# A row-maximum kernel that skips NaNs: VectorE write-back of two quarter rows in tile 62, and a rewritten choice of the engine that writes back

## The chip, the cores and the metric

The kernel runs on one core of a Trainium2 chip. The metric is device time in microseconds; the kernel before takes 1250.19 us (median of three runs, 1250.16 to 1250.23). Engines are named as in the profile: ACT is ScalarE, POOL is GpSimd, DVE is VectorE, SP is SyncE, which issues the DMAs. TensorE has no work.

## What is computed

```python
batch, seq, dim = 32, 2048, 2048
x = np.random.randn(batch, seq, dim).astype(np.float32)
x[np.random.rand(batch, seq, dim) < 0.1] = np.nan
np.nanmax(x, axis=-1).astype(np.float32)
```

There are 65,536 rows of 2048 floats, 536.87 MB in all, and one float per row comes out. Each of the 128 partitions gets 512 whole rows.

## The kernel before

**Tiles.** A tile is up to 7 rows per partition (`WIDE`), that is 28 quarter rows of 512 elements (`Q`), 14336 floats per partition and 7168 KB over the 128 partitions. The table `TILES` lists 75 tiles. An entry has three lists of quarter rows: the loads (one DMA each), the steps and the maxima. Tile n lies in `xt0`, `xt1` or `xt2`, in turn, and the load of a tile waits for the last maximum of the tile that had the buffer before it (line 482, `free`). SP issues the loads in the order of the table (line 240).

**Steps.** A NaN must lose against every number before VectorE takes a maximum. Only the upper 16 bits of each float are touched, seen as a signed integer with a stride of two. First ACT computes a 16-bit key of every element (`act`, line 265, called on line 419): the upper half is mirrored at `TOP` = 0x7F7F with a Prelu whose steep negative branch sends a NaN so far that it comes back as minus infinity. The keys go to one of three key buffers `kt0` to `kt2` of 6144 elements (`KEYS`, `NKEYS`); a step that doesn't fit behind the earlier one takes the next key buffer, and then ACT waits until the keys in it have been written back. Then a second engine mirrors the keys again and writes them over the upper halves in `xt`: the write-back. A positive number in a step is written back by POOL (`pool`, line 275), a negative one by ACT (`release`, line 392, which issues a second ACTIVATE with the function Copy). `[9, 12, -7]` thus has three keys on ACT, two write-backs on POOL and one on ACT. A tuple puts several write-backs behind one key instruction. A float only says when ACT's write-back is issued, or, if positive, that the part joins the one before it.

The line that decides between the engines is 431, `back, wait, c = c < 0, isinstance(c, float), int(abs(c)) * Q`, and line 435, `if back:`.

**Maxima.** DVE takes the maximum of each finished row (`TENSOR_REDUCE`, lines 285 and 458) as soon as the write-backs that cover it are done. Where a maximum needs one write-back of each engine, `joints` (line 90) gives the two a semaphore of their own, so that DVE waits once.

**Order.** Every engine does its instructions in the order in which the loop over the tiles issues them; nothing is scheduled later. In the profile, an instruction's line is that of its helper: L269 is `act`, L279 is `pool`, L286 is `dve`, L245 is a load. Keys read `kt<-xt`, write-backs read `xt<-kt`. DVE's results go to `acc` for the first 60 tiles, then to `lead`. At the end DVE and POOL turn rows without any number to NaN (lines 288 and 300), and SP stores the results.

Of the 75 tiles, the first 57 are mostly `[7, 9, 12]`, with one `[9, 12, -7]` in every eight up to tile 41. Tiles 59 to 61 are `[8, 8, 8, -4]` (the last with the 4 in a tuple), tile 62 is `[7, 10, 11]`, and from tile 63 on most tiles have one or more negative numbers. The last ten are loaded in ever smaller pieces.

One name matters for the change: `tile_nanmax_kernel` begins with aliases, among them line 205, `ACT = mybir.ActivationFunctionType`.

Of the kernel before, what the change touches and what calls it, by code (L numbers as in the profile page):

```python
# [8 lines left out]
D = 2048  # L9

Q = D // 4
# [21 lines left out]
    + [([28], [7, 10, 11], [12, 16])]  # L33
    + [([28], [8, 8, 8, -4], [8, 8, 8, 4])] * 2
# [25 lines left out]

ALONE = (65,)

KEYS = 3 * D
NKEYS = 3

# [6 lines left out]
TOP = 0x7F7F  # L72
NAN = 0x7FC0
LOW = -128

EDGE = TOP + 0.25
# [2 lines left out]


def total(pieces):
    return sum(sum(map(abs, p)) if isinstance(p, tuple) else abs(p) for p in pieces)


def with_last(c):

    return isinstance(c, float) and c > 0


def joints(pieces, reds):  # L90

    flat = []
    at = 0
    for step, parts in enumerate(pieces):
        for c in parts if isinstance(parts, tuple) else (parts,):  # L100

            if with_last(c):
                flat[-1] = (flat[-1][0], at + abs(c), False, step)
            else:
                flat.append((at, at + abs(c), c < 0, step + isinstance(c, float)))
            at += abs(c)
    needs = []
    done = 0
    for n in reds:
        over = [i for i, (a, b, _, _) in enumerate(flat) if a < done + n and b > done]  # L110
        done += n
        pools = [i for i in over if not flat[i][2]]
        backs = [i for i in over if flat[i][2]]
        if pools and backs and flat[pools[-1]][3] > flat[backs[-1]][3]:
            backs = []
        needs.append(pools[-1:] + backs[-1:])
    pairs = {}
    for need in needs:
        if len(need) == 2 and all(sum(i in n for n in needs) == 1 for i in need):
            for i in need:  # L120
                pairs[i] = tuple(need)
    return pairs
# [61 lines left out]
def kernel(  # L184
# [15 lines left out]
    nc = tc.nc  # L200
    P = nc.NUM_PARTITIONS
    f32, i32 = mybir.dt.float32, mybir.dt.int32
    i16, u16 = mybir.dt.int16, mybir.dt.uint16
    ALU = mybir.AluOpType
    ACT = mybir.ActivationFunctionType
# [12 lines left out]
    def sbuf(name, width, dtype):  # L218
        return nc.alloc_sbuf_tensor(name, [P, width], dtype).ap()
# [5 lines left out]
    xts = [sbuf(f"xt{i}", WIDE * D, i32) for i in range(BUFS)]  # L225
    kts = [sbuf(f"kt{i}", KEYS, u16) for i in range(NKEYS)]
    acc0 = sbuf("acc", early, f32)

    def maxima(lo, hi):

# [23 lines left out]
    with tc.tile_critical():  # L254
        xg = xr[P * rows[-1] : P * (rows[-1] + rows[0])].rearrange("(p s) d -> p (s d)", p=P)
        ahead = []
        base = 0
# [7 lines left out]
    def act(deps, pair=None, **kw):  # L265
        return order.add(
            "act",
            nc.scalar,
            lambda: nc.scalar.activation(**kw),  # L269
            deps,  # L270
            lane=pair,
            joint=pair is not None,
        )
# [11 lines left out]
    def dve(deps, do, **kw):  # L285
        return order.add("dve", nc.vector, lambda: do(**kw), deps)  # L286
# [36 lines left out]
    clock = 0  # L323
# [3 lines left out]
        return list({back: e for back, _, e in sorted(uses, key=lambda u: u[1])}.values())  # L327

    key = 0
    used = KEYS  # L330
    number = 0
    stores = []
# [3 lines left out]
    for gi, (s, g) in enumerate(zip(rows, GROUPS)):  # L336
# [6 lines left out]
        acc = maxima(first, first + s)  # L343
        base = 0
        for loads, pieces, reds in g:
            assert sum(loads) == total(pieces) == sum(reds)
            xt, before = xts[number % BUFS], free[number % BUFS]
            number += 1
            landed = []
            at = 0  # L350
            for c in loads:
                c *= Q
                if ahead:
                    e = ahead.pop(0)
# [4 lines left out]
            clean = []  # L359
# [15 lines left out]
            def cleaned(a, b, k, i, e):  # L375

                nonlocal clock
                clock += 1
                both = [(a, b, k, flat[i] < 0, clock)]
                if i in pairs:  # L380
                    if pairs[i] not in half:
                        half[pairs[i]] = both
                        return
                    both += half.pop(pairs[i])
                for a, b, k, back, when in both:
                    kfree[k].append((back, when, e))
                    clean.append((a, b, e))
# [4 lines left out]
            def release():  # L392
                for a, b, k, kp, e, i in held:
                    e = act(
                        [e],
                        name(i),
                        out=xt[:, a:b].bitcast(i16)[:, 1::2],
                        in_=kp,
                        func=ACT.Copy,
                        bias=float(TOP),  # L400
                        scale=-1.0,
                    )
                    cleaned(a, b, k, i, e)
                held.clear()

            for parts in pieces:
                parts = parts if isinstance(parts, tuple) else (parts,)
                c = int(sum(map(abs, parts))) * Q
                here = [l for a, b, l in landed if a < at + c and b > at]
                kold = []  # L410
                if used + c > KEYS:
                    key = (key + 1) % NKEYS
                    used = 0
                    kold, kfree[key] = last(kfree[key]), []
                    assert all(k != key for q in half.values() for _, _, k, _, _ in q)
                    if at + c == sum(loads) * Q and number not in ALONE:

                        kold = kold + last(kfree[(key + 1) % NKEYS])
                e_key = act(
                    here + kold,  # L420
                    out=kts[key][:, used : used + c],
                    in_=xt[:, at : at + c].bitcast(i16)[:, 1::2],
                    func=ACT.Prelu,
                    bias=EDGE,
                    scale=-1.0,
                    alpha=float(TOP - LOW) / (EDGE - NAN),
                )
                release()
                for c in parts:
                    on = more.pop(0)  # L430
                    back, wait, c = c < 0, isinstance(c, float), int(abs(c)) * Q
                    kp = kts[key][:, used : used + c]
                    used += c
                    at += c
                    if back:
                        held.append((at - c, at, key, kp, e_key, piece))
                        if not wait or at == sum(loads) * Q:
                            release()
                    else:
                        group.append((at - c, used - c, key))  # L440
                        if not on:
                            assert all(k == key for _, _, k in group)
                            lo, klo, _ = group[0]
                            e = pool(
                                [e_key],
                                name(piece),
                                out=xt[:, lo:at].bitcast(i16)[:, 1::2],
                                in0=kts[key][:, klo:used],
                                scalar1=-1.0,
                                scalar2=float(TOP),  # L450
                                op0=ALU.mult,
                                op1=ALU.add,
                            )
                            group = []
                            cleaned(lo, at, key, piece, e)
                    piece += not on
                    open_ = [h[0] for h in held + group] + [p[0] for q in half.values() for p in q]
                    while reds and done + reds[0] <= min([at] + open_):
                        n = reds.pop(0)


                        lo = done - 1 if done % D else done
                        done += n
                        row = (base + lo) // D
                        if done % D:
                            m, to = 1, xt[:, done - 1 : done].bitcast(f32)
                        else:
                            m = max(n // D, 1)
                            to = acc[:, row : row + m]
                        e = dve(  # L470
                            [e for a, b, e in clean if b > lo and a < done] + part,
                            nc.vector.tensor_reduce,
                            out=to,
                            in_=xt[:, lo:done]
                            .bitcast(f32)
                            .rearrange("p (c d) -> p c d", c=m),
                            axis=mybir.AxisListType.X,
                            op=ALU.max,
                        )
                        part = [e] if done % D else []  # L480
                        after.append(e)
            free[(number - 1) % BUFS] = after[-1:]
            base += at
        stores.append((og, acc.bitcast(i32)))
# [13 lines left out]
    for (og, bits), e in zip(stores, ready):  # L498
# [6 lines left out]
            step=16,  # L505
# [38 lines left out]
```

## Time and profile before

| what | value |
|---|---|
| median of three runs | 1250.19 us |
| the profiled execution, its own time | 1250.19 us |
| its span, first to last instruction | 1248.9 us |
| data read | 536.87 MB, 430 GB/s over the span |
| write-backs on POOL (`xt<-kt`, L279) | 237 instructions, 1161.1 us |
| write-backs on ACT (`xt<-kt`, L269) | 32 instructions, 61.8 us |
| keys on ACT (`kt<-xt`, L269) | 256 instructions, 914.1 us |

In the profile's groups, the numbers behind the bar are the busy time and the mean of one instruction in ns; behind the second bar stands the idle time of the engine just before these instructions, and what ended it. A timeline row has start and length in us, and in brackets the idle time before it. A row of the windows gives, for a stretch, the busy time and the number of instructions of DVE, ACT and POOL.

### The profile page before, as it was taken

What the parts mean: (1) busy time and instruction counts of PE and PEld (TensorE: products, weight loads), DVE (VectorE), ACT (ScalarE), POOL (GpSimd) and SP (SyncE); (2) the same over time, 40 slices, a digit from 0 to 9 for tenths busy, and PEclk for the clock granted to TensorE, in tenths of its full rate; (3) what the DMA queues carried; (4) which work ended last, traced back from release to release, by engine and by line L of the source; (5) the groups of instructions that cost most, each with busy time, mean ns of one, the idle gap of its engine ahead of it and who ended that gap; (6) DMA issues with size and microseconds to landing.
All of it is one profiled execution on the core that took longest, in us unless ns stands there. A gap on an engine that the chain in (4) does not pass through costs nothing.

```text
span 1248.9 us, 918 instructions
## 1 busy us (share of the span) xinstructions
DVE 1110.2 (89%) x183; ACT 974.4 (78%) x290; POOL 1162.3 (93%) x243
## 2 busy tenths in 40 slices
DVE  0888989888889888898988888988888998999999
ACT  3777887778777877788777877777777789989998
POOL 2999989998999899998999899999999989999898
DMA  9999999999999999999999999999999999999998
GB/s 416 439 415 439 441 441 426 426 441 441 433 419 441 441 433 421 439 441 439 430 424 441 439 435 419 441 441 433 422 437 441 437 434 419 437 428 431 433 426 327
DMA packets 17720, 537.21 MB, mean 430 GB/s; under 512 B 2736, under 2 KB 2736, under 8 KB 5552
## 3 DMA queue, kind: packets, MB, share of 16 engines
q1 hardware_dynamic: 17712, 537.14, 99.6%
q14 instruction: 8, 0.07, 0.0%
HBM read 536.87 MB, written 0.26 MB: 430 GB/s over the span
## 4 chain that ended last, share of the span: by engine, by line
DVE 37%; DMA 36%; POOL 16%; ACT 9%; issue 2%; SPq 0%
DMA xt<-in_x_dram 36%; DVE acc L286 23%; POOL xt L279 16%; DVE lead L286 14%; ACT kt L269 8%; ACT xt L269 1%; SPq L245 0%; SPq L263 0%; SPq L254 0%
## 5 line engine op out<-in xcount | busy, mean ns | idle before, releaser
L279 POOL TENSOR_SCALAR xt<-kt 128x6144 int16<-128x6144 uint16 (+9 forms) x237 | 1161.1, 4899 | 83.2 <-ACT kt L269 69.4
L269 ACT ACTIVATE kt<-xt 128x6144 uint16<-128x6144 int16 (+11 forms) x256 | 914.1, 3610 | 266.3 <-DMA xt<-in_x_dram 245.6
L286 DVE TENSOR_REDUCE acc<-xt 128x3 f32<-128x6144 f32 (+4 forms) x123 | 896.3, 7329 | 129.8 <-POOL xt L279 122.5
L286 DVE TENSOR_REDUCE lead<-xt 128x1 f32<-128x2048 f32 (+3 forms) x57 | 213.2, 3812 | 4.0 <-POOL xt L279 3.9
L269 ACT ACTIVATE xt<-kt 128x512 int16<-128x512 uint16 (+4 forms) x32 | 61.8, 1932 | 0.7
L269 ACT ACT_TABLE_LOAD x1 | 1.3, 1283 | 3.3 <-PEq L263 3.3
L318 DVE MEMSET lead<- 128x1 f32 x1 | 0.1, 59 | 3.4 <-PEq L263 3.4
L279 POOL TENSOR_SCALAR lead<-lead 128x91 int32<-128x91 f32 x1 | 0.6, 552 | 0.1
L286 DVE SCALAR_TENSOR_TENSOR acc<-acc 128x414 f32<-128x414 f32 x1 | 0.6, 592 | 0.0
L314 POOL TENSOR_TENSOR lead<-lead 128x91 int32<-128x91 int32 x1 | 0.4, 377 | 0.1
L525 POOL MEMSET const-float32-0.0<- 128x1 f32 x1 | 0.1, 99 | 0.2 <-issue 0.2
L269 ACT ACTIVATE lead<-lead 128x1 f32<-128x1 f32 x1 | 0.2, 203 | 0.0
L286 DVE SCALAR_TENSOR_TENSOR lead<-lead 128x7 f32<-128x7 f32 x1 | 0.2, 167 | 0.0
L525 POOL MEMSET const-bfloat16-1.0<- 128x1 bf16 x1 | 0.1, 102 | 0.0
L525 POOL MEMSET const-uint8-127<- 128x1 uint8 x1 | 0.1, 102 | 0.0
L525 POOL MEMSET const-float32-1.0<- 128x1 f32 x1 | 0.1, 99 | 0.0
## 6 DMA issues: line engine op xcount, KB each, us to landing
xt<-in_x_dram SPq DMA_DIRECT2D x61, 7168.0 KB, 22.6
xt<-in_x_dram SPq DMA_DIRECT2D x3, 4096.0 KB, 18.1
xt<-in_x_dram SPq DMA_DIRECT2D x5, 2048.0 KB, 30.6
xt<-in_x_dram SPq DMA_DIRECT2D x3, 3072.0 KB, 25.0
xt<-in_x_dram SPq DMA_DIRECT2D x8, 1024.0 KB, 29.1
xt<-in_x_dram SPq DMA_DIRECT2D x3, 2560.0 KB, 22.4
xt<-in_x_dram SPq DMA_DIRECT2D x2, 3584.0 KB, 23.3
xt<-in_x_dram SPq DMA_DIRECT2D x3, 2304.0 KB, 26.2
```

What stands on the lines that cost most here:

```text
L269: lambda: nc.scalar.activation(**kw),
L279: lambda: nc.gpsimd.tensor_scalar(**kw),
L286: return order.add("dve", nc.vector, lambda: do(**kw), deps)
L314: lambda: nc.gpsimd.tensor_tensor(out=bits, in0=bits, in1=none, op=ALU.add),
L318: e_warm = order.add("dve", nc.vector, lambda: nc.vector.memset(warm, 1.0), [])
L525: nc = _bacc.Bacc("TRN2", target_bir_lowering=False, num_devices=1)
```

## The change

The diff, cut to its core:

```diff
-    + [([28], [7, 10, 11], [4, 12, 12])]
+    + [([28], [8, 10, 2j, 8], [8, 12, 8])]
...
+OWN = D
...
+POOL, ACT, DVE = range(3)
+
+
+def backer(c):
+
+    return DVE if isinstance(c, complex) else ACT if c < 0 else POOL
...
-        pools = [i for i in over if not flat[i][2]]
-        backs = [i for i in over if flat[i][2]]
+        pools = [i for i in over if flat[i][2] == POOL]
+        backs = [i for i in over if flat[i][2] == ACT]
...
+    own = nc.alloc_psum_tensor("own", [P, OWN], i32).ap()
...
-                both = [(a, b, k, flat[i] < 0, clock)]
+                both = [(a, b, k, backer(flat[i]), clock)]
...
+                if isinstance(parts[0], complex):
+                    e = act(
+                        here + own_free,
+                        out=own[:, :c],
+                        in_=xt[:, at : at + c].bitcast(i16)[:, 1::2],
+                        func=ACT.Prelu,
...
+                    release()
+                    e = dve(
+                        [e],
+                        nc.vector.tensor_scalar,
+                        out=xt[:, at : at + c].bitcast(i16)[:, 1::2],
+                        in0=own[:, :c],
...
+                    maxima_to(at)
+                    continue
...
-                    back, wait, c = c < 0, isinstance(c, float), int(abs(c)) * Q
+                    by, wait, c = backer(c), isinstance(c, float), int(abs(c)) * Q
...
-                    if back:
+                    if by == ACT:
                         held.append((at - c, at, key, kp, e_key, piece))
                         if not wait or at == sum(loads) * Q:
                             release()
                     else:
                         group.append((at - c, used - c, key))
```

An imaginary number marks a step of a third kind: ACT writes its keys as 32-bit integers to a tensor in PSUM, `own`, and DVE writes them back from there. Only tile 62 has one, of two quarter rows. The loop that issues the maxima has moved, unchanged, into a function `maxima_to`. The engine that writes back is now a number, 0, 1 or 2, that `backer` returns.

The new module-level `ACT` is 1. Inside `tile_nanmax_kernel`, however, the alias of line 205 has the same name and hides it, so `by == ACT` compares a number with the class of activation functions. `joints` and `backer` stand outside that function and see the 1. What this makes of the program is seen in the order of the instructions.

The first place is tile 9, the first whose steps are `[9, 12, -7]`, and the tile behind it. POOL before, with tile 9 in `xt2` and tile 10 in `xt0`:

```order
L279 TENSOR_SCALAR xt2<-kt1 128x4608
L279 TENSOR_SCALAR xt2<-kt2 128x6144
L279 TENSOR_SCALAR xt0<-kt1 128x3584
L279 TENSOR_SCALAR xt0<-kt2 128x4608
L279 TENSOR_SCALAR xt0<-kt0 128x6144
```

POOL at the same place in the changed program:

```order
L290 TENSOR_SCALAR xt2<-kt1 128x4608
L290 TENSOR_SCALAR xt2<-kt2 128x6144
L290 TENSOR_SCALAR xt2<-kt0 128x3584
L290 TENSOR_SCALAR xt0<-kt1 128x3584
L290 TENSOR_SCALAR xt0<-kt2 128x4608
```

The write-back of 7 quarter rows, 3584 elements, has come from ACT to POOL, ahead of the next tile's first one.

The second place is ACT in tiles 61 to 63 (`xt0`, `xt1`, `xt2`). Before:

```order
L269 ACTIVATE kt1<-xt0 128x4096
L269 ACTIVATE kt2<-xt0 128x4096
L269 ACTIVATE kt0<-xt0 128x6144
L269 ACTIVATE xt0<-kt0 128x2048
L269 ACTIVATE kt1<-xt1 128x3584
L269 ACTIVATE kt2<-xt1 128x5120
L269 ACTIVATE kt0<-xt1 128x5632
L269 ACTIVATE kt1<-xt2 128x2048
L269 ACTIVATE kt2<-xt2 128x6144
L269 ACTIVATE xt2<-kt1 128x2048
```

ACT at the same place in the changed program:

```order
L280 ACTIVATE kt1<-xt0 128x4096
L280 ACTIVATE kt2<-xt0 128x4096
L280 ACTIVATE kt0<-xt0 128x6144
L280 ACTIVATE kt1<-xt1 128x4096
L280 ACTIVATE kt2<-xt1 128x5120
L280 ACTIVATE own<-xt1 128x1024
L280 ACTIVATE kt0<-xt1 128x4096
L280 ACTIVATE kt0<-xt2 128x2048
L280 ACTIVATE kt1<-xt2 128x6144
```

ACT's two write-backs (`xt0<-kt0`, `xt2<-kt1`) are gone, and the key to `own` is new.

The third place is POOL in the same three tiles. Before:

```order
L279 TENSOR_SCALAR xt0<-kt1 128x4096
L279 TENSOR_SCALAR xt0<-kt2 128x4096
L279 TENSOR_SCALAR xt0<-kt0 128x4096
L279 TENSOR_SCALAR xt1<-kt1 128x3584
L279 TENSOR_SCALAR xt1<-kt2 128x5120
L279 TENSOR_SCALAR xt1<-kt0 128x5632
L279 TENSOR_SCALAR xt2<-kt2 128x6144
L279 TENSOR_SCALAR xt2<-kt0 128x6144
```

POOL there in the changed program:

```order
L290 TENSOR_SCALAR xt0<-kt1 128x4096
L290 TENSOR_SCALAR xt0<-kt2 128x4096
L290 TENSOR_SCALAR xt0<-kt0 128x4096
L290 TENSOR_SCALAR xt0<-kt0 128x2048
L290 TENSOR_SCALAR xt1<-kt1 128x4096
L290 TENSOR_SCALAR xt1<-kt2 128x5120
L290 TENSOR_SCALAR xt1<-kt0 128x4096
L290 TENSOR_SCALAR xt2<-kt0 128x2048
L290 TENSOR_SCALAR xt2<-kt1 128x6144
L290 TENSOR_SCALAR xt2<-kt2 128x6144
```

The two 2048-element write-backs now stand on POOL, and tile 62 has 13312 elements there in place of 14336. The same holds for the whole program: the changed one has no `xt<-kt` on ACT at all. ACT's 32 write-backs are 32 more on POOL (270 TENSOR_SCALARs on it in place of 238), ACT has one key more, to `own`, and DVE one TENSOR_SCALAR, `xt1<-own 128x1024`, between the first and the second maximum of tile 62. SP's queue is the same.

More of the change, by code (lines that the diff above doesn't have):

```diff
@@ L81, in total @@
 def total(pieces):
-    return sum(sum(map(abs, p)) if isinstance(p, tuple) else abs(p) for p in pieces)
+    return sum(int(abs(c)) for p in pieces for c in (p if isinstance(p, tuple) else (p,)))
 def with_last(c):
     return isinstance(c, float) and c > 0
+POOL, ACT, DVE = range(3)
+def backer(c):
+    return DVE if isinstance(c, complex) else ACT if c < 0 else POOL
 def joints(pieces, reds):
@@ L102, in joints @@
             if with_last(c):
-                flat[-1] = (flat[-1][0], at + abs(c), False, step)
+                flat[-1] = (flat[-1][0], at + int(abs(c)), POOL, step)
             else:
-                flat.append((at, at + abs(c), c < 0, step + isinstance(c, float)))
-            at += abs(c)
+                flat.append((at, at + int(abs(c)), backer(c), step + isinstance(c, float)))
+            at += int(abs(c))
     needs = []
@@ L329 @@
     key = 0
+    own_free = []
     used = KEYS
@@ L404, in release, with maxima_to @@
                 held.clear()
+            def maxima_to(at):
+                nonlocal done, part
+                open_ = [h[0] for h in held + group] + [p[0] for q in half.values() for p in q]
+                while reds and done + reds[0] <= min([at] + open_):
+                    n = reds.pop(0)
+                    lo = done - 1 if done % D else done
+                    done += n
+                    row = (base + lo) // D
+                    if done % D:
+                        m, to = 1, xt[:, done - 1 : done].bitcast(f32)
+                    else:
+                        m = max(n // D, 1)
+                        to = acc[:, row : row + m]
+                    e = dve(
+                        [e for a, b, e in clean if b > lo and a < done] + part,
+                        nc.vector.tensor_reduce,
+                        out=to,
+                        in_=xt[:, lo:done]
+                        .bitcast(f32)
+                        .rearrange("p (c d) -> p c d", c=m),
+                        axis=mybir.AxisListType.X,
+                        op=ALU.max,
+                    )
+                    part = [e] if done % D else []
+                    after.append(e)
@@ L406 @@
             for parts in pieces:
                 parts = parts if isinstance(parts, tuple) else (parts,)
-                c = int(sum(map(abs, parts))) * Q
+                c = total((parts,)) * Q
                 here = [l for a, b, l in landed if a < at + c and b > at]
+                if isinstance(parts[0], complex):
[4 more added lines that the diff above has]
+                        func=ACT.Prelu,
+                        bias=EDGE,
+                        scale=-1.0,
+                        alpha=float(TOP - LOW) / (EDGE - NAN),
+                    )
+                    release()
+                    e = dve(
+                        [e],
+                        nc.vector.tensor_scalar,
+                        out=xt[:, at : at + c].bitcast(i16)[:, 1::2],
+                        in0=own[:, :c],
+                        scalar1=-1.0,
+                        scalar2=float(TOP),
+                        op0=ALU.mult,
+                        op1=ALU.add,
+                    )
+                    clean.append((at, at + c, e))
+                    own_free = [e]
+                    more.pop(0)
+                    piece += 1
+                    at += c
+                    maxima_to(at)
+                    continue
@@ L456 @@
                     piece += not on
[L457 to L481, printed above, removed]
+                    maxima_to(at)
             free[(number - 1) % BUFS] = after[-1:]
```

## The prediction, made before the changed kernel ran

> **What bounds the kernel now.** I read the page first: busy times, DMA slices, groups.
>
> ```profile
> span 1248.9 us, 918 instructions
> DVE 1110.2 (89%) x183; ACT 974.4 (78%) x290; POOL 1162.3 (93%) x243
> DMA  9999999999999999999999999999999999999998
> GB/s 416 439 415 439 441 441 426 426 441 441 433 419 441 441 433 421 439 441 439 430 424 441 439 435 419 441 441 433 422 437 441 437 434 419 437 428 431 433 426 327
> L279 POOL TENSOR_SCALAR xt<-kt 128x6144 int16<-128x6144 uint16 (+9 forms) x237 | 1161.1, 4899 | 83.2 <-ACT kt L269 69.4
> L269 ACT ACTIVATE xt<-kt 128x512 int16<-128x512 uint16 (+4 forms) x32 | 61.8, 1932 | 0.7
> ```
>
> The DMA engines never rest, so before the change the loads set the pace. POOL is next: 93% busy. The change (its order of instructions) puts ACT's 32 write-backs, 61.8 us, on POOL as well, which has 83.2 us of idle time. Whether that is enough depends on where the idle time lies, so I read two stretches of the windows, cut at the last write-back of 4096 elements in tile 61 (1035.12 us):
>
> ```profile
> 1035.12:1245.90 210.78, 207.17 (x56) 198.68 (x98) 197.17 (x64) 1.00 0.99 420
> 1000.00:1035.12 35.12, 34.75 (x11) 29.66 (x10) 29.43 (x7) 1.00 1.01 439
> ```
>
> From 1035.12 to its last instruction POOL is busy for 197.17 us of 210.78: 13.6 us idle. The groups of that stretch, by form, say what comes to it there (ACT's write-backs from 1035 us on):
>
> ```profile
> L269 ACT ACTIVATE xt<-kt 128x2048 int16<-128x2048 uint16 x4 | 9.9, 2479 | 0.0
> L269 ACT ACTIVATE xt<-kt 128x1024 int16<-128x1024 uint16 x7 | 9.4, 1340 | 0.1
> L269 ACT ACTIVATE xt<-kt 128x512 int16<-128x512 uint16 x11 | 8.5, 769 | 0.2
> L269 ACT ACTIVATE xt<-kt 128x3584 int16<-128x3584 uint16 x1 | 4.2, 4213 | 0.0
> L269 ACT ACTIVATE xt<-kt 128x1536 int16<-128x1536 uint16 x2 | 3.8, 1922 | 0.1
> ```
>
> That is 25 instructions and 35.8 us for 13.6 us of room. POOL must end later than the loads.
>
> **The last 210 us, the main term.** A write-back costs the same on either engine, as the groups of the whole span on POOL show beside ACT's rows:
>
> ```profile
> L279 POOL TENSOR_SCALAR xt<-kt 128x6144 int16<-128x6144 uint16 x61 | 429.6, 7043 | 5.2 <-ACT kt L269 0.5
> L279 POOL TENSOR_SCALAR xt<-kt 128x3584 int16<-128x3584 uint16 x51 | 214.1, 4199 | 45.9 <-ACT kt L269 44.7
> L279 POOL TENSOR_SCALAR xt<-kt 128x1024 int16<-128x1024 uint16 x10 | 13.4, 1338 | 0.9 <-ACT kt L269 0.2
> L279 POOL TENSOR_SCALAR xt<-kt 128x512 int16<-128x512 uint16 x3 | 2.3, 764 | 0.2
> ```
>
> 3584 elements take 4199 ns here and 4213 there, 512 take 764 and 769. So 35.8 us are added. [...]
>
> Tile 62 gives something back. two of POOL's rows there, and the mean of its 4096-element ones in the whole span:
>
> ```profile
> L279 POOL TENSOR_SCALAR xt<-kt 128x5632 int16<-128x5632 uint16 x1 | 6.5, 6494 | 0.1
> L279 POOL TENSOR_SCALAR xt<-kt 128x3584 int16<-128x3584 uint16 x1 | 4.2, 4206 | 1.4 <-ACT kt L269 1.4
> L279 POOL TENSOR_SCALAR xt<-kt 128x4096 int16<-128x4096 uint16 x11 | 52.7, 4789 | 6.4 <-ACT kt L269 5.9
> ```
>
> It had 3584 + 5120 + 5632 elements and gets 4096 + 5120 + 4096: 6.49 + 4.21 − 2 × 4.79 = 1.1 us less. Between two of its instructions that wait for nothing, POOL has 0.08 us ("issue" in the chain of waits, next fence). The stretch becomes 197.2 + 35.8 − 1.1 + 88 gaps × 0.08 = **238.9 us** where it was 210.8 to POOL's last end: **28.1 us more**, if nothing makes POOL wait. I take no wait, since the engines that feed it and follow it have room: ACT falls to 198.7 − 35.8 + 1 = 164 us of 239, DVE has 208 of 239, and a load that is issued later, because its buffer comes free later, finds two more tiles in the other buffers for POOL to work on.
>
> **The first 1000 us.** Five tiles `[9, 12, -7]` give POOL 4.20 us more each. Here is the first of them, tile 9, with tile 10 behind it, in the timeline:
>
> ```profile
> 141.11 9.26 ACT L269 ACTIVATE kt<-xt 128x4608 uint16<-128x4608 int16 x2 [4.08 <-DMA xt<-in_x_dram]
> 145.23 12.46 POOL L279 TENSOR_SCALAR xt<-kt 128x4608 int16<-128x4608 uint16 x2 [1.03 <-ACT kt L269]
> 158.00 7.12 ACT L269 ACTIVATE kt<-xt 128x3584 uint16<-128x3584 int16 x2
> 158.06 10.82 DVE L286 TENSOR_REDUCE acc<-xt 128x5 f32<-128x10240 f32 x1 [1.47 <-ACT xt L269]
> 161.27 16.74 POOL L279 TENSOR_SCALAR xt<-kt 128x3584 int16<-128x3584 uint16 x3 [3.58 <-ACT kt L269]
> 174.90 7.12 ACT L269 ACTIVATE kt<-xt 128x3584 uint16<-128x3584 int16 x2 [4.07 <-DMA xt<-in_x_dram]
> ```
>
> and from the chain of waits:
>
> ```profile
> 165.47 0.08 issue
> ```
>
> POOL ends tile 9's second write-back at 157.69 and then idles 3.58 us. The moved one fills that: 157.69 + 0.08 + 4.20 = 161.97, so tile 10 starts at 162.05 in place of 161.27, 0.8 us late. A plain tile takes POOL 16.74 + 0.08 = 16.82 us, and loads land every 16.90 us (174.90 − 158.00), so the lag shrinks by 0.08 us a tile and is mostly gone after seven. POOL's lag alone costs nothing here.
>
> The load can pay, though. Tile 9's last maximum waits for that write-back: 162.0 + 10.82 = 172.8 in place of 168.9, and then SP issues tile 12's load, while tile 11 lands at 174.88, 2.0 us later. Is 2.0 us enough to keep the DMA queues full? The trace has no load that is issued so late, save the first one, into empty queues, and the stores:
>
> ```profile
> 0.95 50.05 SPq L245 DMA_DIRECT2D xt<-in_x_dram  x5
> 5.75 1.91 ACT L269 ACTIVATE kt<-xt 128x2048 uint16<-128x2048 int16 x1 [0.95 <-DMA xt<-in_x_dram]
> out_dram<-lead SPq DMA_DIRECT2D x1, 45.5 KB, 1.5
> ```
>
> The first load's 1024 KB arrive 4.8 us after issue, 2.4 us of them at 434 GB/s: 2.4 us of overhead, 0.35 us too much, 1.7 us in five tiles. A store has at most 1.5 us: nothing lost. I take **1.2 us**, nearer to the load's end since it is the same kind of transfer, and keep 0 and 1.7. [...]
>
> Tiles 59 to 61, `[8, 8, 8, -4]`: by the second window row POOL is idle 5.7 us of 35.1, seven gaps of 0.08 among them, and gets two write-backs of 2.48 + 0.08 before 1035.12. That fits with nothing to spare; I add **0.3 us** of lag (0 to 0.4, since the third key of tile 61 itself waits for POOL).
>
> **What costs nothing.** DVE's new TENSOR_SCALAR, 1024 integers out of PSUM, has no row; the nearest are the maximum of 2048 floats, 2278 ns, and the 414-element SCALAR_TENSOR_TENSOR, 592 ns. I take 1.2 us, between them; the 31 us that DVE has free in the stretch hide it, and if POOL were not behind, it would cost these 0.6 to 2.3 us. [...] ACT's key to PSUM (1041 ns for 1024 elements to a key buffer) is hidden in the same way. ACT's 35.8 us that go are no gain: nothing late waits for ACT alone.
>
> **The end and the sum.** The last lines of the timeline:
>
> ```profile
> 1243.44 1.33 POOL L279 TENSOR_SCALAR xt<-kt 128x1024 int16<-128x1024 uint16 x1
> 1242.74 4.47 DVE L286 TENSOR_REDUCE lead<-xt 128x1 f32<-128x2048 f32 x2
> 1247.25 0.17 DVE L286 SCALAR_TENSOR_TENSOR lead<-lead 128x7 f32<-128x7 f32 x1
> ```
>
> Behind POOL's last data (1244.77) come a maximum, the search for empty rows and a store, as now, only that DVE will be waiting already: 0.1 us less. Span: 1248.9 + 28.1 + 1.2 + 0.3 − 0.1 = 1278.4. The profiled execution took 1250.19 in all, 1.3 more than its span, and that is the median of the runs too. **Forecast: 1279.7 us.**
>
> **The rivals.**
>
> *Keys become the wait.* If POOL still waits for ACT as often in the last 210 us as now, its waits stay on top:
>
> ```profile
> POOL xt L279 <- ACT kt L269: 10.0, 15, 1.9
> ```
>
> Up to 10.0 us, 1290. For it: ACT must wait for POOL to free a key buffer, and a tile's last key waits for two. Against it: those waits came from POOL having caught up with the loads, and ACT has 75 us to spare. 8%; with half of the waits kept it is 1285.
>
> *The main stage runs away.* If POOL kept the 0.2 us that it waits at the start of a tile,
>
> ```profile
> 42.81 16.75 POOL L279 TENSOR_SCALAR xt<-kt 128x3584 int16<-128x3584 uint16 x3 [0.22 <-ACT kt L269]
> ```
>
> its tile would be 17.04 us against 16.90: it would not recover, and lose 0.14 us in some 50 tiles and 0.8 in five: 11 us in place of 1.2, 1289. Against it: that wait is for a load that has just landed, and vanishes when POOL is late. 6%.
>
> *Not slower.* POOL's 83.2 us of idle time swallow 61.8 + 32 × 0.08 = 64.4 us, and the loads still set the end: 1250, at best 1.1 less for tile 62's relief. It decides if POOL could have worked ahead, with 37 us idle after 1035 us; it has 13.6. 2%.
>
> *The change does what it says.* If ACT kept its write-backs, only tile 62 would change: POOL 1.1 us shorter in a stretch where the loads set the pace, so 1249 to 1250.5. The order shows no write-back on ACT. 2%.
>
> **How the numbers follow.** The forecast has 82%; its own bounds are 1278 (no DMA loss, no lag) to 1281, with 1 us below for gaps and tail. The range goes to 1284 for the nearer part of the rivals. A change under 0.2% (2.5 us) can't be told from none; both low rivals fall there, 3% with 1% for faster, and slower keeps 96%.
>
> **What would show it.** In the changed profile: no `xt<-kt` on ACT; POOL x275 with about 1223 us busy and no idle after 1037 us; the last load landing within 2 us of now (1243 us), the chain's last 230 us on POOL instead of DVE, and DMA slices thinning only near the end. If POOL waits for ACT there, the first rival holds; if loads land ever later before 1000 us, the second. I am wrong altogether if POOL's write-backs get faster or slower in a row.

## The result, and the profile after

The changed kernel takes 1284.65 us (median of four runs, 1283.48 to 1285.32) against 1250.18 us: a ratio of 1.0274, 95% interval 1.0262 to 1.0286. The forecast was 1279.7 us, the range went to 1284.0: right in sign and in the larger part of the 34 us, some 5 us short. The profiled execution took 1283.48 us and is the fastest of the four, so 1.2 us of the distance to the median can't be seen in it. Its page:

```profile
span 1282.2 us, 920 instructions
DVE 1113.7 (87%) x184; ACT 914.8 (71%) x259; POOL 1221.3 (95%) x275
GB/s 405 431 453 433 429 424 430 431 431 419 435 433 431 428 429 431 429 431 426 433 429 429 429 429 429 433 445 437 431 430 429 431 433 433 433 431 431 428 389 7
POOL 45%; DMA 30%; DVE 18%; ACT 6%; issue 1%; SPq 0%
L290 POOL TENSOR_SCALAR xt<-kt 128x6144 int16<-128x6144 uint16 (+9 forms) x269 | 1220.2, 4536 | 57.6 <-ACT kt L280 39.8
```

The helper lines have moved: L280 is `act`, L290 is `pool`, L297 is `dve`, L256 is a load. POOL has 32 instructions more, there is no group `xt<-kt` on ACT, and the last slice of the span moves 7 GB/s: the loads are over and POOL is still at work. In the chain of waits POOL's share is now the largest.

The stretch from the last 4096-element write-back of tile 61 to POOL's last instruction, and the start of that write-back, from the windows and the timeline:

```profile
1041.27:1279.28 238.01, 211.02 (x57) 164.50 (x74) 231.03 (x89) 1.00 0.87 372
1041.27 12.15 POOL L290 TENSOR_SCALAR xt<-kt 128x4096 int16<-128x4096 uint16 x3 [0.42 <-ACT kt L280]
```

89 instructions, 231.0 us busy, 238.0 us long: the forecast had 89 and 238.9 us. But the stretch begins at 1041.27 us, where the forecast had 1036.6. The missing 4.7 us were lost before it. The waits behind 1042 us say that nothing was lost after it:

```profile
ACT kt L280 <- POOL xt L290: 48.0, 18, 9.6
DVE lead L297 <- POOL xt L290: 27.2, 33, 3.1
ACT kt L280 <- DMA xt<-in_x_dram: 4.7, 2, 2.8
POOL xt L290 <- ACT kt L280: 0.4, 1, 0.4
```

Both neighbours wait for POOL now, and POOL for almost nothing (the columns are the total in us, the number of waits and the longest); its one wait is the 0.42 us in front of the write-back at 1041.27.

Where the 4.7 us went is seen at the load of tile 12, which takes the buffer of tile 9, the first `[9, 12, -7]`. SP's row and ACT's rows for tiles 11 and 12 after the change:

```profile
172.77 0.33 SPq L256 DMA_DIRECT2D xt<-in_x_dram  x1
174.85 3.19 ACT L280 ACTIVATE kt<-xt 128x3584 uint16<-128x3584 int16 x1 [3.33 <-DMA xt<-in_x_dram]
193.88 7.12 ACT L280 ACTIVATE kt<-xt 128x3584 uint16<-128x3584 int16 x2 [5.53 <-DMA xt<-in_x_dram]
```

and SP and tile 12 before it:

```profile
168.91 0.33 SPq L245 DMA_DIRECT2D xt<-in_x_dram  x1
191.87 7.13 ACT L269 ACTIVATE kt<-xt 128x3584 uint16<-128x3584 int16 x2 [4.14 <-DMA xt<-in_x_dram]
```

The load is issued at 172.77 us, within 0.1 us of what the forecast worked out, 2.05 us before tile 11's load lands (ACT starts on that at 174.85, at once). Tile 12 then follows tile 11 by 19.03 us, where 16.90 is the rule: 2.1 us lost, not 0.35. By the landings in the trace, the loads of tiles 12, 20, 28, 36 and 44, each issued 2.0 to 2.1 us ahead, lose 2.1, 1.1, 1.3, 0.7 and 0.8 us, together **6.1 us** where the forecast took 1.2. Tile 61, whose last write-back opens the stretch, lands 5.9 us later than before (1027.0 us against 1021.1); the loads between them vary by some tenths and make up the difference.

### The profile page after: what moved, and what is told of

Read it like the earlier page. It is cut to its first block, busy times and chain, and to the rows that moved or that the text cites. A ratio compares the mean times of both kernels' runs of the same rounds, so it can differ in the third digit from the quotient of the medians.

```text
span 1282.2 us, 920 instructions
## 1 busy us (share of the span) xinstructions
DVE 1113.7 (87%) x184; ACT 914.8 (71%) x259; POOL 1221.3 (95%) x275
## 4 chain that ended last, share of the span: by engine, by line
POOL 45%; DMA 30%; DVE 18%; ACT 6%; issue 1%; SPq 0%
POOL xt L290 45%; DMA xt<-in_x_dram 30%; DVE acc L297 18%; ACT kt L280 6%; DVE lead L297 0%; SPq L256 0%; SPq L274 0%; SPq L265 0%
## 5 line engine op out<-in xcount | busy, mean ns | idle before, releaser
L290 POOL TENSOR_SCALAR xt<-kt 128x6144 int16<-128x6144 uint16 (+9 forms) x269 | 1220.2, 4536 | 57.6 <-ACT kt L280 39.8
L280 ACT ACTIVATE kt<-xt 128x6144 uint16<-128x6144 int16 (+10 forms) x256 | 912.4, 3606 | 340.2 <-DMA xt<-in_x_dram 265.7
L297 DVE TENSOR_REDUCE acc<-xt 128x3 f32<-128x6144 f32 (+4 forms) x123 | 895.8, 7328 | 136.3 <-POOL xt L290 136.3
L297 DVE TENSOR_REDUCE lead<-xt 128x1 f32<-128x2048 f32 (+3 forms) x57 | 215.8, 3817 | 27.3 <-POOL xt L290 27.2
L297 DVE TENSOR_SCALAR xt<-own 128x1024 int16<-128x1024 int32 x1 | 1.3, 1298 | 0.0
L280 ACT ACTIVATE own<-xt 128x1024 int32<-128x1024 int16 x1 | 1.0, 1009 | 0.0
L297 DVE SCALAR_TENSOR_TENSOR acc<-acc 128x414 f32<-128x414 f32 x1 | 0.7, 746 | 0.0
L290 POOL TENSOR_SCALAR lead<-lead 128x91 int32<-128x91 f32 x1 | 0.5, 549 | 0.1
L280 ACT ACTIVATE lead<-lead 128x1 f32<-128x1 f32 x1 | 0.2, 203 | 0.0
L297 DVE SCALAR_TENSOR_TENSOR lead<-lead 128x7 f32<-128x7 f32 x1 | 0.2, 167 | 0.0
## 6 DMA issues: line engine op xcount, KB each, us to landing
xt<-in_x_dram SPq DMA_DIRECT2D x3, 2560.0 KB, 13.6
```

Of the source, the lines that this page charges most:

```text
L290: lambda: nc.gpsimd.tensor_scalar(**kw),
```

## The experiments

Three explanations were set against each other. **A**: the loads that are issued too late cost the 6 us, by how little ahead of the landing before them they are issued (the *lead*). **B**: a late issue costs what the first load's overhead says, and the rest has another cause. **C**: POOL's own lag, the work moved to it in the five tiles, is what delays tile 61.

**e1_named_apart**: the comparison is made with the number that was meant, so ACT keeps its write-backs and only tile 62 is new.

```diff
-                    if by == ACT:
+                    if by == 1:
```

> The changed kernel with the comparison made against the number 1, so that ACT keeps its 32 write-backs and only tile 62 is new. Theory (the slowdown is the write-backs that moved to POOL, not tile 62's new step): 1249.5 to 1250.7 us, with POOL's 25 extra instructions after 1035 us gone. Rival (the PSUM step holds something up, or DVE reading PSUM slows POOL): above 1252 us.

1250.35 us against 1250.48 us (the kernel before is measured again beside each group of experiments: 1250.48, 1250.53 and 1250.44 us), ratio 1.0 (0.999 to 1.0009). Tile 62's step through PSUM costs and gains nothing that can be told; all of the 34 us is the write-backs' move.

**e2_main_only**: the kernel before, with only the five early write-backs moved.

```diff
-    + [([28], [9, 12, -7], [8, 20])]
+    + [([28], [9, 12, 7], [8, 20])]
```

> The kernel before, with the five tiles [9, 12, -7] made [9, 12, 7]: only their write-backs of 3584 elements move to POOL, the last 210 us are as before. Theory A (the loads are issued some 2 us before the queues run dry, and that costs 0.7 to 2.1 us each time): 1255 to 1257 us, with loads 12, 20, 28, 36, 44 landing late, and the whole loss seen at the end since the loads set it. Rival B (a late issue costs what the first load's overhead says, 0.35 us each): 1250.5 to 1252 us. Rival C (the delay at 1036 us comes from POOL's lag, not from the loads): below 1251 us, since POOL catches up in the tail.

1257.25 us (1255.87 to 1258.95), ratio 1.0055 (1.004 to 1.007): 6.8 us more: just above A's range, and well above B's and C's. The five loads lose 1.6, 0.6, 1.0, 1.5 and 1.0 us at leads of 2.0 to 2.3 us. The write-back in tile 61 starts late as well, and the end moves with the loads:

```profile
1040.70 4.75 POOL L279 TENSOR_SCALAR xt<-kt 128x4096 int16<-128x4096 uint16 x1 [0.33 <-ACT kt L269]
```

**e3_tail_only**: the changed kernel, but ACT keeps its write-backs in the first 49 tiles.

```diff
-                    if by == ACT:
+                    if by == (1 if number < 50 else ACT):
```

> The changed kernel, but in the first 49 tiles ACT keeps its write-backs; from tile 59 on they are on POOL. Theory A: the 28 us of the last stretch and some 0.3 us of lag alone, 1278 to 1279.5 us. Rivals B and C (the five early tiles cost little through the loads): 1282 us or more.

1277.92 us (1277.83 to 1277.98), ratio 1.022: 27.4 us more, 0.1 us below A's range, and far from the 1282 us of B and C. POOL reaches the same write-back early:

```profile
1035.79 7.31 POOL L290 TENSOR_SCALAR xt<-kt 128x4096 int16<-128x4096 uint16 x2 [0.42 <-ACT kt L280]
POOL 37%; DMA 33%; DVE 20%; ACT 9%; issue 1%; SPq 0%
```

1035.79 against 1035.12 before, 0.7 us later; half of that is POOL's lag in tiles 59 to 61, as shown further down. 6.8 + 27.4 = 34.2 us, the whole change within 0.3 us: the two terms add.

**e4_split_maximum**: the changed kernel with the same work on POOL, but in the five tiles the last maximum is cut, so that the buffer comes free sooner.

```diff
-    + [([28], [9, 12, -7], [8, 20])]
+    + [([28], [9, 12, -7], [8, 12, 8])]
```

> The changed kernel, with the maxima of the five tiles [9, 12, -7] split 8, 12, 8 in place of 8, 20: the same work on POOL, but the last maximum is 4.4 us instead of 10.8, so the buffer comes free 6.4 us earlier and the load is issued some 8 us ahead of the landing before it. Theory A: the early loss goes, 1278 to 1279.5 us, POOL's piece of tile 61 back at 1035.3 to 1036 us. Rival C (POOL's lag in the five tiles): no change, 1284 us.

1277.99 us (1277.96 to 1278.15), as in e3. The load of tile 12 is issued at 168.75 us, 6.3 us ahead (not 8: DVE takes the middle maximum until 164.4 and the last one behind it):

```profile
168.75 0.33 SPq L256 DMA_DIRECT2D xt<-in_x_dram  x1
191.94 7.12 ACT L280 ACTIVATE kt<-xt 128x3584 uint16<-128x3584 int16 x2 [3.43 <-DMA xt<-in_x_dram]
1035.90 7.32 POOL L290 TENSOR_SCALAR xt<-kt 128x4096 int16<-128x4096 uint16 x2 [0.42 <-ACT kt L280]
```

All seven quarter rows are still on POOL in these tiles and nothing is lost. That rules out C: what cost 6.7 us was the issue of five loads, 4 us earlier or later. The runs agree with one another again, too: they differ by 0.2 us here and by 1.8 us in the changed kernel, whose losses vary from load to load.

The next runs vary the lead, all on the kernel before, with nothing else changed than the five tiles.

**e6_lead_0**: the maxima 4 and 24, so that the last one ends 2.2 us later than in e2.

```diff
-    + [([28], [9, 12, -7], [8, 20])]
+    + [([28], [9, 12, 7], [4, 24])]
```

> The kernel before with the five tiles [9, 12, 7] and their maxima 4, 24: POOL's work as in the run of the early tiles alone, but the last maximum takes 13.0 us, so the load is issued when the one before it lands (lead 0). Theory A (what counts is how far ahead of the landing a load is issued, and 2.0 us ahead loses 1.2 us): 1.2 + 2.1 = 3.3 us each, 1265 to 1269 us. Rival B (the first load's overhead of 2.4 us alone): 2.4 us each, 1262 us. Rival C (POOL's lag): as the early tiles alone, 1257 us.

1264.16 us (1263.86 to 1264.63), ratio 1.011: 13.6 us more. SP issues tile 12's load 0.1 us after tile 11's has landed:

```profile
174.96 3.19 ACT L269 ACTIVATE kt<-xt 128x3584 uint16<-128x3584 int16 x1 [3.28 <-DMA xt<-in_x_dram]
175.06 0.33 SPq L245 DMA_DIRECT2D xt<-in_x_dram  x1
194.79 3.19 ACT L269 ACTIVATE kt<-xt 128x3584 uint16<-128x3584 int16 x1 [6.30 <-DMA xt<-in_x_dram]
```

Each of the five loses 2.6 to 3.2 us, mean 2.9. The time lies between A's 1265 and B's 1262. Here, with the queues really empty, B's rule is nearly right: the overhead is 2.8 us (2.9 − 0.1) against the 2.4 of the first load. C falls again, since POOL's work is that of e2.

**e9_lead_2_6** and **e7_lead_3**: only 6 or 5 of the 7 quarter rows move (the first and the second line added).

```diff
-    + [([28], [9, 12, -7], [8, 20])]
+    + [([28], [9, 12, (6, -1)], [8, 20])]
...
+    + [([28], [9, 12, (5, -2)], [8, 20])]
```

> The same with [9, 12, (6, -1)]: lead 2.65 us. Theory A with a limit near 2.4 us: 1250.5 us. Theory A with a limit near 4 us: 0.8 to 1.3 us each, 1254 to 1257 us. Rival C: 6/7 of the loss, 1256 us.

> The kernel before with the five tiles [9, 12, (5, -2)]: 5 of the 7 quarter rows move to POOL, so the last maximum starts 1.2 us earlier than with all 7 and the lead is 3.2 us. Theory A with a limit near 2.4 us: no loss, 1250.5 us. Theory A with a limit near 4 us (the first late load of the changed kernel took 4.2 us longer than its transfer): 0.5 to 1 us each, 1253 to 1255 us. Rival C: about 5/7 of the loss of all seven, 1255 us.

1256.38 us (1256.01 to 1258.49) and 1255.18 us (1255.09 to 1256.13), 5.9 and 4.7 us more. A limit near 2.4 us is out. C's proportion would fit these two by themselves; e4 and e6 had ruled it out, and the next pair does so on C's own ground.

**e10_lead_3_8** and **e11_lead_4_9**: 4 or 2 of the 7 move.

```diff
-    + [([28], [9, 12, -7], [8, 20])]
+    + [([28], [9, 12, (4, -3)], [8, 20])]
...
+    + [([28], [9, 12, (2, -5)], [8, 20])]
```

> The kernel before with the five tiles [9, 12, (4, -3)]: 4 quarter rows move to POOL, lead 3.8 us. Theory A (a load must be issued some 4 to 5 us before the one ahead lands): a small loss, 0.2 to 0.6 us each, 1251.5 to 1253.5 us. Rival C (the loss follows the work moved to POOL): 4/7 of 6.8 us, 1254.4 us.

> The same with [9, 12, (2, -5)]: lead 4.9 us. Theory A: no loss, 1250.5 us, 1251 at most. Rival C: 2/7 of 6.8 us, 1252.5 us.

1251.68 us (1250.93 to 1253.12), ratio 1.0012 (1.0002 to 1.0021), and 1251.01 us, ratio 1.0005 (0.9995 to 1.0015). C wanted 1254.4 and 1252.5. The 0.6 us that e11 has over the kernel before lie inside its interval, but no run of the one overlaps one of the other (1250.86 to 1251.12 and 1250.25 to 1250.69); its five loads lose nothing, and where this comes from no run shows. At 3.7 to 4.0 us of lead a load loses 0.1 us on average, at 4.9 to 5.2 us nothing:

| kernel | lead of the five loads, us | mean loss of one, us | least and most | time over before, us |
|---|---|---|---|---|
| before | 5.9 to 6.0 | 0.0 | 0.0, 0.1 | 0 |
| e11 | 4.9 to 5.2 | 0.0 | 0.0, 0.0 | 0.6 |
| e10 | 3.7 to 4.0 | 0.1 | 0.0, 0.3 | 1.2 |
| e7 | 3.2 to 3.4 | 0.9 | 0.1, 1.8 | 4.7 |
| e9 | 2.6 to 2.7 | 1.2 | 0.2, 2.3 | 5.9 |
| e2 | 2.0 to 2.3 | 1.1 | 0.6, 1.6 | 6.8 |
| the change | 2.0 to 2.1 | 1.2 | 0.7, 2.1 | (34.5) |
| e6 | −0.1 | 2.9 | 2.6, 3.2 | 13.6 |

(Lead: from the issue to the landing of the load ahead; loss: distance of the two landings less 16.90 us; both from the profiled execution, while the last column has the medians.)

**e8_tail_old_62**: as e3, with tile 62 as it was.

```diff
-    + [([28], [8, 10, 2j, 8], [8, 12, 8])]
+    + [([28], [7, 10, 11], [4, 12, 12])]
```

> The kernel in which only the write-backs from tile 59 on moved, with tile 62 as it was, [7, 10, 11] and maxima 4, 12, 12: without the step to PSUM. Theory (POOL sets the end, and each of its instructions counts): POOL has 1.1 us more, so 1277.9 + 1.1 = 1279.0 us. Rival (the step to PSUM changes nothing or costs something): 1277.9 us or less.

1279.33 us (1279.24 to 1279.74), 1.4 us above e3. Where POOL sets the end, two quarter rows that DVE takes over are worth about what they cost on POOL (1.1 us by the rows); in e1, where the loads set it, they are worth nothing.

## Why the prediction was wrong, step by step

- **ACT's 32 write-backs go to POOL**: right, and the whole cause (e1).
- **The last 210 us, 28.1 us more**: right. The stretch measured 238.0 us in place of 238.9, as POOL was busy for 231.0 us in place of 231.9; e3 with the lag included gives 27.4 us. No wait stayed in it: POOL waited for ACT once, 0.4 us, in front of its first instruction. The first rival (keys become the wait) is out.
- **Tile 62, 1.1 us off POOL**: 1.4 us (e8).
- **DVE's new instruction, 1.2 us and hidden**: 1298 ns, hidden where POOL sets the end. In e1 POOL isn't behind, and there the prediction would have charged 0.6 to 2.3 us; nothing is seen (1250.35 against 1250.48 us). The row of the changed kernel:

```profile
L297 DVE TENSOR_SCALAR xt<-own 128x1024 int16<-128x1024 int32 x1 | 1.3, 1298 | 0.0
```

- **POOL's lag in the early tiles costs nothing by itself**: right (e4). It does shrink, by 0.07 us from tile 10 to tile 11 in the changed kernel (POOL starts on them 4.02 and 3.95 us after ACT does, where it took 3.27 before), and it is gone in tile 12, whose load lands late. The second rival, a main stage that runs away, did not happen: between the late loads, the landings stay at 16.9 us.
- **The late loads, 0 to 1.7 us, taken as 1.2: the step that failed.** The place, the cause and the moment of the issue were right (172.8 us forecast, 172.77 measured); the price was 6.1 us. So the last load landed at 1248.7 us, and not within 2 us of 1243. I had taken the first load's 2.4 us of overhead as the whole condition: a load issued 2.05 us ahead would lose 0.35 us. That holds about for queues that are empty (e6: 2.8 us of overhead). For queues that are still at work a lead of 2 to 3.4 us, which should have lost 0.35 us or nothing, lost 0.9 to 1.2 us on average and up to 2.3. Of these 7168 KB loads, those with 3.7 to 4.0 us of lead lost 0.1 us on average (e10), and those with 4.9 to 5.2 us nothing (e11).
- **Tiles 59 to 61, 0.3 us (0 to 0.4)**: right. Tile 61's last write-back starts 13.97 us after the tile has landed before the change (1021.15 and 1035.12 us), 14.24 in the changed kernel (1027.03 and 1041.27) and 14.31 in e3 (1021.48 and 1035.79). The lag is 0.3 us, and the rest of e3's 0.7 us is a load that lands 0.3 us later there, as ACT's first keys of the tile show (before, then e3):

```profile
1021.23 7.12 ACT L269 ACTIVATE kt<-xt 128x4096 uint16<-128x4096 int16 x2 [1.77 <-DMA xt<-in_x_dram]
1021.57 7.12 ACT L280 ACTIVATE kt<-xt 128x4096 uint16<-128x4096 int16 x2 [4.45 <-DMA xt<-in_x_dram]
```

- **The end**: the tail behind POOL is 2.9 us, as forecast.

In the profiled execution the errors add up: the write-back of tile 61 is 6.15 us late (5.88 by the loads, 0.27 by the lag) in place of 1.5, the stretch 0.9 us shorter than forecast, so 1278.4 + 4.65 − 0.9 = 1282.2 us, the measured span.

What stays open is why a load issued 2 to 3.4 us ahead loses anything. The trace shows that it isn't the load as a whole that is late. A load has 16 parts that land separately; those of tile 11 land within 0.45 us, those of tile 12 within 2.3 us, and thirteen of the sixteen by 192.3 us, the other three between 193.1 and 193.9. The last one sets the landing.

The trace also has every single DMA packet. A part is eight packets of 57,344 bytes, one behind the other, and in a load that is issued in time (tile 12 in e11) each takes 2.12 us and a part starts as soon as the one ahead of it ends. In tile 12 of the changed kernel some of the 16 parts start late, 3.8 us in all, and the first packets are slow: 2.57 us on average and up to 3.1, the seven behind them 2.13. In e7, at 3.2 us of lead, the late starts come to 0.6 us in all, yet four of the first packets take 2.6 to 4.1 us, and the load lands 1.8 us late. So a load can lose time although hardly any queue has run empty; why its first packets are slow, no run here tells.

## What to carry to other kernels

A buffer that came free 2.0 us before the load ahead had landed wasn't in time here: a load lost 1.2 us on average. For loads that set the pace, read how long before the landing of the load ahead each one is issued, and take anything under the smallest lead that the trace shows to be harmless (4.6 us, tile 37 of the changed kernel; at the 3.7 to 4.0 us of e10 up to 0.3 us were lost) as a loss, not only what lies under the start-up time of a first load (2.4 us). A cheap cure is to shorten the last instruction that frees the buffer: splitting the last maximum of five tiles got 6.7 us back with no work removed. And a sum of idle time over the span (83 us here) says nothing on where the work to be moved falls (36 us into 13.6).

## What was unexpected of the hardware

- Empty queues cost 2.9 us from landing to landing over the usual 16.9 us (e6), and queues with 2 us of work left still 1.2 us in the changed kernel and 1.1 in e2, with a scatter from 0.6 to 2.1 us between loads that are issued alike. Part of it is first packets that take 2.6 to 2.8 us on average in the changed kernel's five late loads, and up to 3.8, where 2.12 is usual.
- The scatter reaches the time: the runs of kernels with such loads differ by up to 3 us (e2: 1255.87 to 1258.95), those without by 0.1 to 0.5 us (e1, e3, e4, e8).
